# Sums of weight quarters made in HBM: the additions moved behind GpSimd's scaling steps, and one sum of the second product made on VectorE

## The chip, the cores and the metric

The kernel runs on one core of one Trainium2 chip. The metric is device time in microseconds (us), the median over the runs. Engines are named as in the profile: PE (TensorE, matrix products), ACT (ScalarE), DVE (VectorE), POOL (GpSimd) and SP (SyncE, which here only issues transfers).

## The reference

One decoder layer on 512 tokens of width 1024, in float32:

```
h = rms_norm(x); proj = h @ w_in                      # u, q, k/v for three branches, gates
y_pool = pool_mixer(u)                                # causal means over 2, 4, 8, 16 tokens
y_nsa  = nsa_mixer(q, k.., v..)                       # 16 heads: compressed + selected + window attention
merged = g_a * (y_pool @ w_proj_pool) + g_b * (y_nsa @ w_proj_nsa)
x = x + merged @ w_out
h = rms_norm(x)
x = x + square(relu(h @ w_ff1)) @ w_ff2               # w_ff1: 1024 x 4096, w_ff2: 4096 x 1024
out = rms_norm(x)
```

With 512 tokens and at most 16 selected blocks of 64, every causal block is selected, so both large attention branches are plain causal softmax. The last three lines but one, the MLP, are where the sums of this case are used; the attention is where they are made.

## The kernel before, in words

**Precision by splitting.** A float32 operand is split into a high part (ACT writes `h`) and a rest (DVE or POOL writes `l = t - h`), and a product is three matmuls: high by high, high by rest, rest by high.

**Stages.** Input projections; attention with the rest of the projections as filler between its steps (the loop at L1080); the projection `w_proj_nsa` and `w_out`; the MLP. The MLP works in four rounds `c` of 1024 hidden features each. A round has a first product (through `w_ff1`, two groups of 512 columns, class `Group`) and, in rounds 0 to 2, a second product (through `w_ff2`, two groups, class `Out`); the second product of round 3 is done plainly.

**Fewer products by sums.** Each group multiplies a 2 x 2 arrangement of quarters with seven quarter products in place of eight (the Strassen-Winograd scheme). The weights' side needs quarters and sums of quarters. With the quarters of a group called A11, A12, A21, A22, the kernel uses A11, A12, A22, S1 = A21 + A22, S3 = A11 + A21, S2 = S1 + A11 and S4 = S2 + A12 (signs are taken care of elsewhere). One quarter product is 24 matmuls of 128 x 256. The order of the products of a first product is `IN_TURN` (L138; `FIRST` in round 0), that of a second product `OUT_TURN` (L139), whose letters stand for the two groups in turn. On the activations' side, DVE and ACT make the sums T1 to T4 of the hidden quarters in `Hidden.sums`; S3 is multiplied with T3, A22 with T4, S2 with T2, A12 with hidden quarter 21, S4 with 22.

**Where the sums are made.** S1, S3 and S2 are made in HBM ahead of time, by two transfers each: SP copies one quarter into a buffer (L259, `S<-w_ff`, or `S<-S` where S2 starts from S1), and then POOL issues a transfer that adds another quarter to it (L255, `accum_op=ALU.add`). `jobs` is the list of them: three for each of the 14 groups, 42 in all. S4 is not loaded but made on DVE in the tile in which S2 was loaded (L296): the dictionary `held` keeps the first of its two terms until the other is there.

**Who issues when.** `emit_load` issues the next 512 KB load of weights on SP (L223); there are 64 loads up to the end of `w_out`, then those of the MLP. After load `i` it calls `make_sum` as often as `sums_after(i)` says: never before load 38, once for loads 38 to 40, twice for loads 41 to 51 (these are issued during attention), then after every third, and in the MLP after every fourth load. Call `n` of `make_sum` issues the addition of job `n - 2` on POOL and the copy of job `n` on SP. An addition waits on POOL until its copy has landed.

**The queues.** Every engine works through its own instructions in the order in which the compiler's scheduler has put them; an instruction whose input is not there holds all that stand behind it. In attention POOL also does, for each of 96 slots (one head, one block of queries), the scaling of the softmax (`weight`, L1007), the weights of the compressed branch (L921 to L924), half of the rests of the weights (L332) and the rotary products (L574, L577). What POOL scales in slot `i`, PE transposes (L1023) four passes of the loop later. A loaded tile (`raw`, five in the MLP: four and `raw5`) is given back for the next load when both parts have been split off.

Of the kernel before, what the change touches and what calls it, by code (L numbers as in the profile page):

```python
# [2 lines left out]

# [1 line left out]

# [11 lines left out]
ALU = mybir.AluOpType  # L17
# [45 lines left out]
def trunk(ctx: ExitStack, tc: tile.TileContext, A, out):  # L63
    nc = tc.nc
    PE, ACT, DVE, POOL = nc.tensor, nc.scalar, nc.vector, nc.gpsimd
# [39 lines left out]
    def add_key(k):  # L105
# [14 lines left out]
        else:  # L120
# [14 lines left out]
    MLP0 = len(LD)  # L135
    C_FF2 = 3
    FIRST = ("A11", "A12"), ("S1", "S3", "S2"), ("A22", "S4")
    IN_TURN = ("A11", "S3", "S1", "S2", "A12", "A22", "S4")  # L138
    OUT_TURN = ("A11", "A11", "S1", "S1", "A12", "A12", "S2", "S4", "S2", "S4", "S3", "S3", "A22", "A22")  # L139
    dp = ctx.enter_context(tc.tile_pool(name="sums", bufs=1, space=bass.MemoryType.DRAM))  # L140
    jobs, late = [], []

    def quarters(layer, c, g):

        w, r, o = ((w_f1, 0, 1024 * c + 512 * g), (w_f2, 1024 * c, 512 * g))[layer - 1]
        return {f"{i + 1}{j + 1}": w[r + 512 * j:r + 512 * j + 512, o + 256 * i:o + 256 * i + 256].rearrange(
            "(k p) c -> p k c", p=128) for i in range(2) for j in range(2)}

    def add_group(layer, c, g):

        q = quarters(layer, c, g)
        of = {"A" + k: v for k, v in q.items()}
        for o in ("S1", "S3", "S2"):
            of[o] = dp.tile([128, 4, 256], F32, name=f"{o}_{layer}{c}{g}")
        jobs.append((of["S1"], q["21"], q["22"]))
        jobs.append((of["S3"], q["11"], q["21"]))
        if late:
            jobs.append(late.pop())
        late.append((of["S2"], of["S1"], q["11"]))
        return of  # L160

    SUM_OF = {}

    def add_turn(layer, c, of, turn):
        for g, o in turn:
            key = f"{o}{layer}{c}{g}"
            if o == "S4":
                WL.append((key, key))
                continue
            if o in ("S2", "A12"):  # L170
                SUM_OF[key] = f"S4{layer}{c}{g}"
            WL.append((key, len(LD)))
            LD.append([(of[g][o], 0)])

    for c in range(4):
        of = [add_group(1, c, g) for g in range(2)]
# [6 lines left out]
        if c < C_FF2:  # L183
            of = [add_group(2, c, g) for g in range(2)]
            seen = {}
            turn = []
            for o in OUT_TURN:
                g = seen.get(o, 0)
# [10 lines left out]
    raws, hls = {}, {}  # L199
    st = {"load": 0, "prep": 0, "use": 0, "kept": 0, "pairs": 0, "sums": 0}  # L200
    spare, slots_hl = [], []
    held = {}

    def emit_load():

        i = st["load"]
        if i >= len(LD):
            return False
        segs = LD[i]
        a = segs[0][0].shape[1]  # L210
        b = sum(s.shape[2] for s, _ in segs)
        assert a * b <= 1024
        if not by_name() or st["kept"] < RAW:
            st["kept"] += by_name()
            t = wp.tile([128, 1024], F32, tag="raw", bufs=RAW, name=f"raw{i}")
        elif spare:
            t = spare.pop(0)
        else:
            return False
        st["load"] += 1  # L220
        v = t[:, :a * b].rearrange("p (a b) -> p a b", a=a)
        for s, o in segs:
            began = nc.sync.dma_start(v[:, :, o:o + s.shape[2]], s)  # L223
        raws[i] = (t, a, b)
        for _ in range(int(sums_after(i))):
            make_sum(began)
        return True

    def sums_after(i):

        p, f = len(P1), len(P1) + len(FILL2)
        if i < p + 3:
            return 0
        if i < f + 4:
            return 1 + (i >= p + 6)
        return i % 3 == 0 if i < MLP0 else i % 4 == 0

    def by_name():

        return st["load"] >= MLP0  # L240
# [5 lines left out]

    def make_sum(load):

        n = st["sums"]
        if n > len(jobs) + 1:  # L250
            return
        st["sums"] += 1
        if n > 1:
            to, _, q = jobs[n - 2]
            POOL.dma_start(to, q, accum_op=ALU.add)  # L255
        if n < len(jobs):
            to, q, _ = jobs[n]
            with tc.issue_after(load.ins):
                nc.sync.dma_start(to, q)  # L259

    part = {}
    mode = {"pool": False, "first": True}
# [201 lines left out]
    GT = ap.tile([128, NT, 48], F32, name="GT")  # L464
# [151 lines left out]
    with ExitStack() as c1:  # L616
# [185 lines left out]
        for k in P1[2:]:  # L802
            i = int(k[-1]) if k[-1].isdigit() else None
# [35 lines left out]
    with ExitStack() as c2:  # L839
# [157 lines left out]
        def weight(i):  # L997
            p, half, br, qb, h = slots[i]
            ps, sm, P = live[i]
            head = 2 * p + h  # L1000
            bl = blocks(i)
            nb_ = len(bl)
            c = 3 * head + 1 + bl[0][0]
            DVE.reciprocal(sm[:, 2, 0:nb_], sm[:, 1, 0:nb_])  # L1004
            for e, (b, o, nb) in enumerate(bl):
                n = 128 * nb
                POOL.tensor_scalar(P[:, o:o + n], P[:, o:o + n], sm[:, 2, e:e + 1], GT[:, qb, c + e:c + e + 1],  # L1007
                                   op0=ALU.mult, op1=ALU.mult)

        def pt_tile(i):  # L1010
            p, half, br, qb, h = slots[i]
# [63 lines left out]
        n = len(slots)  # L1075
# [4 lines left out]
        for i in range(n + LAG + PLAG):  # L1080
            if i < n:
                p = slots[i][0]
                if i % 12 == 3 and p + 1 < NPAIR:
                    while p + 1 not in Q:
                        fill()
                        step_side()
                if i % 12 == CMP_AT and p + 1 < NPAIR:
                    side.append(cmp_scores(p + 1))
            if i + 1 < n:
                score_pe(i + 1)  # L1090
                scored["pairs"] = (i + 2) // 12
            t = i - LAG
            if 0 <= t < n:
                turn_pe(t)
                turn_hi(t)
            if i < n:
                smax(i)
                expo(i)
            if 0 <= i - 1 < n:
                weight(i - 1)  # L1100
            if 0 <= t < n:
                turn_lo(t)
            step_side()
            want = done0 + (total - done0) * (i + 1) // (n + LAG + PLAG)
            while fdone[0] < want and fill():
                pass
            if i < 5:
                fill()
            j = t - PLAG
            if 0 <= j < n and j % 2 == 1 and pv(j):  # L1110
                o_evac(*slots[j][0:2])
# [368 lines left out]
    for c in range(4):  # L1480
# [16 lines left out]
        if c < C_FF2:  # L1497
            outs = [Out(c, h, Y) for h in range(2)]
            seen = {}
            for o in OUT_TURN:  # L1500
                h = seen.get(o, 0)
# [5 lines left out]
        else:  # L1507
# [10 lines left out]
            last = NT - 1  # L1518
            o = MA[:, 2 * last:2 * last + 2, :].rearrange("p j c -> p (j c)")
# [43 lines left out]
```

## Time and profile before

| | |
|---|---|
| median of 3 runs | 832.32 us (832.32, 828.6, 832.45) |
| the profiled execution's own time | 832.95 us |
| its span, first to last instruction | 831.1 us |
| what lies around the span | 1.85 us |
| mean granted TensorE clock | 0.987 |
| HBM read and written | 131.53 MB and 46.14 MB |

A wait row gives the waiting engine, line and tile, what released it, and then the sum in us, the number of waits and the longest. A timeline row gives start, duration, engine, line, operation, and in brackets the idle time before it and who ended it. A window row gives the length of the stretch, the busy time of PE, PE's weight loads, DVE, ACT and POOL with their number of instructions, the granted clock of TensorE, the busy share of the 16 DMA engines and GB/s. PE's matmuls overlap: a 128 x 256 one is listed with 0.28 us though the next starts about 0.12 us after it.

### The profile page before, as it was taken

The numbers are of one execution on the slowest core, as the hardware profiler recorded it, in microseconds if no ns is written. First come the engines' busy times: TensorE is split into PE (matmuls) and PEld (weight loads), VectorE is DVE, ScalarE is ACT, GpSimd is POOL, SyncE is SP. The second block draws the span as 40 slices with busy tenths as digits, with TensorE's granted clock in tenths as the row PEclk, the third lists the DMA queues.
The fourth block names the chain that finished last, engine by engine and source line by source line (L and its number), as shares of the span: only waits on it lengthen the run. The fifth ranks groups of instructions, "written<-read, shape, count | busy, mean of one in ns | idle before, by whom it ended". The sixth has DMA issues, their size and how long they took to land.

```text
span 831.1 us, 13946 instructions
## 1 busy us (share of the span) xinstructions
PE 797.0 (96%) x5081; PEld 712.2 (86%) x5081; DVE 613.8 (74%) x1195; ACT 484.0 (58%) x959; POOL 215.0 (26%) x277
## 2 busy tenths in 40 slices
PE   7999999987998999999999899999999999999997
PEld 6889878875876888888788689999999999999986
DVE  7796744535978788989565659897789778987823
ACT  6576533334976787889633447764675467436811
POOL 6000000026767788785233300010110000000000
PEclk9999999997999899999999999999999999999999
DMA  9464633389439878673696803979987944365402
GB/s 292 120 179 114 166 90 105 106 183 230 74 97 248 164 159 187 145 151 58 220 236 179 241 11 102 284 185 279 243 252 181 274 148 158 109 197 178 152 1 101
DMA packets 125502, 137.15 MB, mean 165 GB/s; under 512 B 5365, under 2 KB 112409, under 8 KB 125210
## 3 DMA queue, kind: packets, MB, share of 16 engines
q1 hardware_dynamic: 102970, 113.46, 42.7%
q0 software_dynamic: 22176, 22.02, 18.4%
q8 instruction: 40, 0.66, 0.3%
q10 hardware_dynamic: 288, 0.79, 0.3%
q14 instruction: 28, 0.23, 0.1%
HBM read 131.53 MB, written 46.14 MB: 214 GB/s over the span
## 4 chain that ended last, share of the span: by engine, by line
PE 69%; DVE 14%; DMA 5%; issue 5%; ACT 4%; POOL 3%; SPq 0%; POOLq 0%; ACTq 0%; DVEq 0%
PE psF L373 19%; PE psB L1332 16%; PE psB L373 12%; PE psB L1448 9%; DMA S<-w_ff 3%; PE psO L1057 3%; PE psT L1023 3%; PE psS L962 2%; PE psV L373 2%; DVE P L984 1%; DVE wl L287 1%; POOL wl L332 1%; PE psF L427 1%; DVE PT L1038 1%; DMA raw<-w_out 1%
## 5 line engine op out<-in xcount | busy, mean ns | idle before, releaser
L373 PE MATMUL psF<-R,wh 128*128 128x512 f32 x512 | 167.4, 405 | 0.2 <-ACT MA L820 0.2
L255 POOL DMA_DIRECT2D S<-w_ff x42 | 53.3, 1269 | 259.1 <-DMA S<-w_ff 132.4
L285 ACT ACTIVATE wh<-raw 128x1024 fp32r<-128x1024 f32 x66 | 69.7, 1057 | 76.8 <-PE psB L1448 32.5
L330 ACT ACTIVATE wh<-raw 128x512 fp32r<-128x512 f32 (+1 forms) x102 | 61.3, 619 | 84.5 <-PE psF L373 35.7
L373 PEld LDWEIGHTS psF<-R,wh 128*128 128x128 f32 x512 | 93.0, 190 | 18.1 <-ACT MA L820 0.5
L1007 POOL TENSOR_SCALAR P<-P,sm,GT 128x128 f32<-128x128 f32 (+3 forms) x128 | 99.1, 977 | 25.2 <-DVE sm L1004 17.3
L373 PE MATMUL psF<-R,wl 128*128 128x512 f32 x256 | 102.2, 399 | 0.7 <-DVE wl L332 0.7
L287 DVE TENSOR_TENSOR wl<-raw,wh 128x1024 fp32r<-128x1024 f32 x66 | 80.5, 1222 | 18.7 <-ACT wh L285 18.4
L332 DVE TENSOR_TENSOR wl<-raw,wh 128x512 fp32r<-128x512 f32 (+1 forms) x78 | 59.0, 768 | 38.1 <-ACT wh L330 37.8
L994 ACT ACTIVATE P<-P,sm 128x128 f32<-128x128 f32 (+3 forms) x128 | 71.1, 557 | 14.6 <-DVE sm L984 11.6
L984 DVE CUSTOM_DVE_ANT_0 P<-psS,cst 128x128 f32<-128x128 f32 (+3 forms) x128 | 59.7, 484 | 13.9 <-PE psT L1023 7.4
L1332 PE MATMUL psB<-R,wh 128*128 128x256 f32 x352 | 64.1, 282 | 0.0
L1034 ACT ACTIVATE PT<-psT 128x512 fp32r<-128x512 f32 (+2 forms) x96 | 49.2, 520 | 25.0 <-PE psT L1023 24.3
L1038 DVE TENSOR_TENSOR PT<-psT,PT 128x512 fp32r<-128x512 f32 (+2 forms) x96 | 56.7, 595 | 9.3 <-ACT PT L1034 8.5
L1023 PE MATMUL psT<-ident,P 128*128 128x128 f32 x320 | 52.9, 280 | 9.0 <-POOL P L1007 8.6
L373 PEld LDWEIGHTS psF<-R,wl 128*128 128x128 f32 x256 | 48.5, 190 | 11.9 <-DVE wl L332 0.9
L1023 PEld LDWEIGHTS psT<-ident,P 128*128 128x128 f32 x320 | 40.3, 143 | 20.9 <-POOL P L1007 12.8
L285 ACT ACTIVATE w3h<-raw 128x1024 fp32r<-128x1024 f32 x32 | 33.8, 1057 | 41.1 <-PE psB L1448 15.9
L1332 PEld LDWEIGHTS psB<-R,wh 128*128 128x128 f32 x352 | 54.1, 189 | 0.3 <-DVE R L1274 0.2
L332 POOL TENSOR_TENSOR wl<-raw,wh 128x512 fp32r<-128x512 f32 x28 | 41.5, 1484 | 35.3 <-ACT wh L330 35.1
L1057 PE MATMUL psO<-PT,VV 128*128 128x256 f32 x320 | 49.3, 290 | 0.4 <-ACT PT L1034 0.4
L1332 PE MATMUL psB<-R,wl 128*128 128x256 f32 x176 | 49.5, 281 | 0.0
(431 smaller groups left out, 2274.3 us busy)
## 6 DMA issues: line engine op xcount, KB each, us to landing
raw<-w_ff SPq DMA_DIRECT2D x50, 512.0 KB, 4.8
S<-w_ff POOLq DMA_DIRECT2D x42, 512.0 KB, 7.8
raw<-S SPq DMA_DIRECT2D x42, 512.0 KB, 4.6
raw<-w_in SPq DMA_DIRECT2D x32, 512.0 KB, 3.9
S<-w_ff SPq DMA_DIRECT2D x28, 512.0 KB, 6.5
S<-S SPq DMA_DIRECT2D x14, 512.0 KB, 6.0
raw<-w_proj_nsa SPq DMA_DIRECT2D x8, 512.0 KB, 4.0
raw<-w_out SPq DMA_DIRECT2D x8, 512.0 KB, 5.0
```

The lines of the kernel that those rows point to most:

```text
L285: ACT.activation(h, t, AF.Copy)
L287: DVE.tensor_tensor(l, t, h.bitcast(F32), op=ALU.subtract)
L332: eng.tensor_tensor(l[:, sl], t[:, sl], h[:, sl].bitcast(F32), op=ALU.subtract)
L373: PE.matmul(ps, a, b, start=first and j == 0, stop=last and j == n - 1, skip_group_check=True)
L984: DVE.tensor_tensor_reduce(out=P[:, o:o + n].rearrange("p (a c) -> p a c", c=128), in0=s, in1=m, scale=1.0, scalar=3e38, op0=ALU.add, op1= ...
L994: last_exp[:] = [ACT.activation(c, c, AF.Exp, bias=sm[:, 0, e:e + 1], scale=-1.0, accum_out=sm[:, 1, e:e + 1])]
L1007: POOL.tensor_scalar(P[:, o:o + n], P[:, o:o + n], sm[:, 2, e:e + 1], GT[:, qb, c + e:c + e + 1], op0=ALU.mult, op1=ALU.mult)
L1023: PE.transpose(pt[:, 128 * j:128 * j + 128], P[:, 128 * j:128 * j + 128], ident)
L1038: DVE.tensor_tensor(dL, src, dH.bitcast(F32), op=ALU.subtract)
L1057: PE.matmul(ps[:, qb % 2, :, :], VV[:, k, b, g, :], t[:, j, :, :], start=False, stop=last and j == len(kbs) - 1 and t is tL, skip_group_ch ...
L1332: PE.matmul(out, w[u][:, k, 128 * f:128 * f + 128], XB[x][v][:, k, :], **kw)
L1448: PE.matmul(out, YB[y][u][:, k, 128 * f:128 * f + 128], w[v][:, k, :], **kw)
```

## The change

The list of jobs gets shorter: groups of the second product no longer have S2 made in HBM (36 jobs, and six loads less). There S2 is made on DVE from the tiles of S3 and A22, since S2 = S1 + A11 = S3 + A22, and S4 from S2 and A12 as before. So S3 and A22 must be multiplied ahead of S2, and `OUT_TURN` puts them fifth to eighth, where A12 and S2 began before.

Copies and additions are no longer issued in one call. `make_sum` now issues only the copy and notes the job in `begun`; `add_sum` issues the addition of the oldest job begun. A copy follows each of loads 38 to 55, none the loads 56 to 63, and in the MLP every third load. In attention an addition is issued after every fourth slot where two jobs or more are begun, and it is ordered behind the last scaling step of that pass (`tc.issue_after` makes it stand behind that instruction in POOL's queue). From load 52 on, an addition goes with a load when more than two jobs are begun. Where a copy starts from a buffer whose addition is still to be issued, that addition is issued first.

```diff
-    OUT_TURN = ("A11", "A11", "S1", "S1", "A12", "A12", "S2", "S4", "S2", "S4", "S3", "S3", "A22", "A22")
+    OUT_TURN = ("A11", "A11", "S1", "S1", "S3", "S3", "A22", "A22", "S2", "A12", "S4", "S2", "A12", "S4")
...
-        for o in ("S1", "S3", "S2"):
+        for o in ("S1", "S3", "S2")[:4 - layer]:
             of[o] = dp.tile([128, 4, 256], F32, name=f"{o}_{layer}{c}{g}")
...
-        late.append((of["S2"], of["S1"], q["11"]))
+        if layer == 1:
+            late.append((of["S2"], of["S1"], q["11"]))
...
-            if o == "S4":
+            to = {"S2": "S4", "A12": "S4"}.get(o) if layer == 1 else {"S3": "S2", "A22": "S2", "S2": "S4", "A12": "S4"}.get(o)
+            if to:
+                SUM_OF[key] = f"{to}{layer}{c}{g}"
+            if o not in of[g]:
                 WL.append((key, key))
                 continue
-            if o in ("S2", "A12"):
-                SUM_OF[key] = f"S4{layer}{c}{g}"
...
-        for _ in range(int(sums_after(i))):
+        if sums_after(i):
             make_sum(began)
+        if i >= len(P1) + len(FILL2) + 4 and (len(begun) > 2 or begun and st["sums"] == len(jobs)):
+            add_sum()
...
     def sums_after(i):
-        p, f = len(P1), len(P1) + len(FILL2)
-        if i < p + 3:
-            return 0
-        if i < f + 4:
-            return 1 + (i >= p + 6)
-        return i % 3 == 0 if i < MLP0 else i % 4 == 0
+        if i < MLP0:
+            return len(P1) + 3 <= i < len(P1) + len(FILL2) + 8
+        return i % 3 == 0
...
     def make_sum(load):
-        n = st["sums"]
-        if n > len(jobs) + 1:
-            return
-        st["sums"] += 1
-        if n > 1:
-            to, _, q = jobs[n - 2]
-            POOL.dma_start(to, q, accum_op=ALU.add)
-        if n < len(jobs):
-            to, q, _ = jobs[n]
+        if st["sums"] < len(jobs):
+            to, q, _ = jobs[st["sums"]]
+            while any(q is jobs[n][0] for n in begun):
+                add_sum()
             with tc.issue_after(load.ins):
                 nc.sync.dma_start(to, q)
+            begun.append(st["sums"])
+            st["sums"] += 1
+
+    def add_sum(behind=None):
+        to, _, q = jobs[begun.popleft()]
+        with tc.issue_after(behind.ins) if behind else nullcontext():
+            POOL.dma_start(to, q, accum_op=ALU.add)
...
             if 0 <= i - 1 < n:
-                weight(i - 1)
+                last = weight(i - 1)
+            if i % 4 == 3 and len(begun) > 1:
+                add_sum(last)
```

More of the change, by code (lines that the diff above doesn't have):

```diff
@@ L1 @@
 from collections import deque
-from contextlib import ExitStack
+from contextlib import ExitStack, nullcontext
 import numpy as np
@@ L201, in trunk @@
     spare, slots_hl = [], []
-    held = {}
+    held, begun = {}, deque()
     def emit_load():
@@ L1006, in weight @@
                 n = 128 * nb
-                POOL.tensor_scalar(P[:, o:o + n], P[:, o:o + n], sm[:, 2, e:e + 1], GT[:, qb, c + e:c + e + 1],
-                                   op0=ALU.mult, op1=ALU.mult)
+                r = POOL.tensor_scalar(P[:, o:o + n], P[:, o:o + n], sm[:, 2, e:e + 1],
+                                       GT[:, qb, c + e:c + e + 1], op0=ALU.mult, op1=ALU.mult)
+            return r
         def pt_tile(i):
```

## The prediction

> **What bounds the kernel now.** I read the page first, then what PE waited for, then the busy time by stage, and last the queues of POOL and PE around each wait. The page's first part, then PE's waits:
>
> ```profile
> PE 797.0 (96%) x5081; PEld 712.2 (86%) x5081; DVE 613.8 (74%) x1195; ACT 484.0 (58%) x959; POOL 215.0 (26%) x277
> ...
> PE psT L1023 <- POOL P L1007: 8.6, 5, 2.9
> PE psB L373 <- DVE wl L332: 3.5, 1, 3.5
> PE psT L932 <- POOL PC L924: 3.3, 1, 3.3
> ```
>
> PE is the bound, and the change takes no matmul from it. What can be won is PE's idle time, 831.1 - 797.0 = 34 us, and time in which PE runs at a lower clock. Of the waits, 8.6 + 3.3 = 11.9 us end with POOL, all in attention. The stages, in windows (three stretches with waits, two without, and the MLP):
>
> ```profile
> 175.00:212.00 37.00, 28.70 (x133) 22.75 (x132) 19.41 (x62) 17.10 (x46) 21.11 (x29) 0.86 0.89 191
> 255.00:280.00 25.00, 20.44 (x115) 16.97 (x115) 19.31 (x60) 16.11 (x42) 16.19 (x22) 0.86 1.05 200
> 280.00:400.00 120.00, 118.74 (x770) 104.18 (x770) 105.85 (x346) 104.23 (x276) 89.15 (x117) 1.00 0.65 143
> 455.00:475.00 20.00, 16.48 (x64) 12.92 (x64) 12.56 (x13) 9.60 (x18) 7.77 (x6) 0.91 0.98 269
> 580.00:660.00 80.00, 79.79 (x671) 79.59 (x670) 66.21 (x79) 45.62 (x61) 6.94 (x6) 1.00 0.86 239
> 660.00:740.00 80.00, 79.80 (x671) 79.59 (x670) 69.38 (x83) 46.02 (x60) 0.00 (x0) 1.00 0.50 160
> 616.00:645.00 29.00, 28.79 (x242) 28.59 (x241) 27.88 (x37) 18.49 (x26) 2.31 (x2) 1.00 0.75 207
> ```
>
> Two stretches of early attention and one at the end of `w_out` lose time: PE idles 8.3, 4.6 and 3.5 us there, at clocks of 0.86, 0.86 and 0.91. Later attention (280 to 400) has none of that, with DVE, ACT and POOL as busy as anywhere. The MLP is full: 671 matmuls in 80 us, in one stretch with sums and in one without. So attention can gain, and the MLP can only lose. What holds POOL in the bad stretches shows in its queue, and beneath it in PE's:
>
> ```profile
> 184.77 1.15 POOL L255 DMA_DIRECT2D S<-w_ff  x1 [8.70 <-DMA S<-w_ff]
> 187.13 0.72 POOL L924 TENSOR_TENSOR PC<-cw,PC 128x256 fp32r<-128x256 f32 x1
> 195.29 1.19 POOL L255 DMA_DIRECT2D S<-w_ff  x1 [6.21 <-DMA S<-w_ff]
> 198.12 1.67 POOL L255 DMA_DIRECT2D S<-w_ff  x1
> 267.29 1.19 POOL L255 DMA_DIRECT2D S<-w_ff  x1 [4.04 <-DVE sm L1004]
> 271.67 1.19 POOL L255 DMA_DIRECT2D S<-w_ff  x1 [2.38 <-DVE PT L1038]
> 446.53 1.15 POOL L255 DMA_DIRECT2D S<-w_ff  x1 [6.08 <-DVE W1L L332]
> ...
> 187.90 0.71 PE L932 MATMUL psT<-identR,PC 128*128 128x128 f32 x4 [3.32 <-POOL PC L924]
> 197.03 0.75 PE L1023 MATMUL psT<-ident,P 128*128 128x128 f32 x2 [2.87 <-POOL P L1007]
> 200.35 0.89 PE L1023 MATMUL psT<-ident,P 128*128 128x128 f32 x2 [1.35 <-POOL P L1007]
> 269.35 0.66 PE L1023 MATMUL psT<-ident,P 128*128 128x128 f32 x4 [2.38 <-POOL P L1007]
> 273.62 0.90 PE L1023 MATMUL psT<-ident,P 128*128 128x128 f32 x3 [1.08 <-POOL P L1007]
> ```
>
> Each wait of PE comes behind an addition (L255) at which POOL stood idle: the scaling that PE needs was queued behind an addition whose copy had not landed. Where a DVE line is named (267.29, 271.67, 446.53), DVE had long been done; the copies were late. The chain of waits has the late one, the copies' landing times (issue to landing, 160 to 280 us: least, median, most) agree, and so does the list of the additions issued from 160 to 400:
>
> ```profile
> 253.47 17.66 DMA S<-w_ff
> ...
> DMA to landing us min/median/max: 4.8/6.7/17.7
> ...
> L255 POOL DMA_DIRECT2D S<-w_ff x25: 1130/1192/1717, 169.6 to 370.7; - x25
> ```
>
> **The change, part by part.**
>
> *Additions in attention.* Before, addition n - 2 is issued with copy n, and two such calls go with one load, so an addition follows its copy by a single load. In bursts that is too soon: at 252.8 two additions hung on copies of a few us before. Counting through the new code, 15 jobs are begun by load 52, and an addition goes out behind the fourth slot only where a newer job is begun: 11 to 14 additions instead of 23 up to load 51, the first four on copies issued before 190, when no slot has run yet. The 102 passes take the time from 188 to about 400, so four passes are some 8 us, longer than the 6.7 us median of a copy. The additions before the first slot, among them that of 184.77, are gone. POOL's own time for an addition, 1.19 us, falls away some ten times in attention; with POOL 89 of 120 us busy in the good stretch that is off the path and counts as nothing. If POOL were the bound it would be worth 12 us.
>
> *PE's idle time in attention.* The five waits shown are 3.32 + 2.87 + 1.35 + 2.38 + 1.08 = 11.0 us. I take all of them; the bounds are 0 (the additions wait as before) and 11.9 (all waits for POOL).
>
> *The clock.* In the two stretches PE was busy 28.70 and 20.44 us at 0.86, so (0.14 x 28.70) + (0.14 x 20.44) = 6.9 us went to the clock. From 280 to 400, where PE idles 1.3 us in 120, the clock is 1.00. Bounds 0 and 6.9; I take 4.8, nearer the upper, since the low clock stands exactly where the waits are. [...]
>
> *The end of w_out.* With loads 56 to 63 no copies go out, and no additions, so the block of 6.08 us before 446.53 is gone. The wait of 3.5 us behind it, with the clock 3.5 + 0.09 x 16.48 = 5.0 us, is the upper bound, 0 the lower, because the loads of `w_out` themselves come one tile behind another. I take 2.0.
>
> *Sums on DVE.* Six S2 sums are new, each like the S4 sums:
>
> ```profile
> L296 DVE TENSOR_TENSOR raw<-raw,raw x14: 1214/1222/1228, 515.2 to 768.3; 128x1024 f32<-128x1024 f32 x14
> ...
> 630.62 0.28 PE L1448 MATMUL psB<-wh,y21H 128*128 128x256 f32 x1
> ...
> 630.99 0.69 DVE L1390 TENSOR_TENSOR yT3L<-GB,yT3H 128x512 fp32r<-128x512 f32 x1
> 632.19 0.69 DVE L1390 TENSOR_TENSOR yT4L<-GB,yT4H 128x512 fp32r<-128x512 f32 x1
> ```
>
> That is 6 x 1.222 = 7.3 us on DVE, the upper bound. Lower bound: 0; a gain is excluded, as PE has no idle time there (79.79 of 80 us). From 616 to 645 DVE is busy 27.88 of 29 us, and the new order asks for T3 at the fifth product of a second product (start 630.62) and for T4 at the seventh, two products or 5.7 us later (80 us for 28). T3 is complete at 631.68, T4 at 632.88: T4 in time, T3's last half about when the second half of the fifth product starts, since that wants k = 0 and 1 first. The two sums at A22 fall in the same saturated stretch, where the old order had the two S4 sums. I take 0.3 us in each of three second products, 1.0 in all.
>
> *Transfers in the MLP.* Six copies, six additions and six loads go; they were hidden. But five more copies and five more additions move in between load 64 and load 120 (20 additions there instead of 15). The rows of one round with sums and one without:
>
> ```profile
> L255 POOL DMA_DIRECT2D S<-w_ff x6: 1156/1156/1158, 584.1 to 652.0; - x6
> ...
> L259 SPq DMA_DIRECT2D S<-S x3: 495/496/505, 589.1 to 645.2; - x3
> L259 SPq DMA_DIRECT2D S<-w_ff x2: 555/555/555, 599.4 to 613.9; - x2
> ...
> L223 SPq DMA_DIRECT2D raw<-S x12: 320/338/342, 581.8 to 650.9; - x12
> L223 SPq DMA_DIRECT2D raw<-w_ff x12: 367/384/392, 593.4 to 659.4; - x12
> ...
> DMA to landing us min/median/max: 3.4/5.4/7.8
> ...
> L223 SPq DMA_DIRECT2D raw<-S x12: 319/338/339, 662.3 to 731.3; - x12
> L223 SPq DMA_DIRECT2D raw<-w_ff x11: 367/383/384, 673.9 to 737.2; - x11
> ```
>
> Without sums 23 loads fill 0.50 x 80 = 40 us of DMA time, 1.74 each. With sums it is 0.86 x 80 = 68.8; less 24 x 1.74 that leaves 27 for six additions and five copies, 4.9 a pair. A first product (40 us) of the new kernel has 12 loads and 4 pairs, 20.9 + 19.6 = 40.5 us, all of it; a second product has 10 loads and 3.3 pairs, 33.6 of 40. The row of 255 to 280 shows 1.05, so it fits, with loads landing later than 5.4 us. Lower bound 0, for the same reason as above; upper bound in the rival below; I take 0.5, as loads are issued four or five ahead. The additions follow their copies by six loads there, POOL has nothing else to do, and every sum is issued at least twelve loads before it is loaded.
>
> *Sum.* -11.0 - 4.8 - 2.0 + 1.0 + 0.5 = -16.3; from the profiled execution's 832.95 us that is 816.6. The median of the runs is 0.6 below that execution, the lowest run 4.3.
>
> **The rivals.**
>
> *The clock stays low.* The waits go, but the low clock of early attention has a cause of its own, so the 4.8 us don't come back: 832.95 - 16.3 + 4.8 = 821.4. For it: the longest of the waits is 3.32 us, yet 0.86 is the mean of 37 us. Against it: the dips lie where the waits are, and nowhere from 280 to 400. Chance 0.10. [...]
>
> *The additions still wait in the burst.* The three loads from 242 to 253 bring three copies within 11 us, and copies then took up to 17.7 us. An addition behind every fourth slot can meet a copy still in flight, and the next scaling stands behind it as now. Then the stretch 255 to 280 keeps its 2.38 + 1.08 us and 70% of its 2.9 us of clock: 816.6 + 5.5 = 822.1. Chance 0.15. If all additions wait so, because the scheduler sets them as early as the order allows, nothing is won but the 2.0 of `w_out`, and the MLP's 1.5 is paid: 832.5. Chance 0.08.
>
> *Slower: the MLP waits for its loads.* In a first product four tiles rotate (one of five is held for S4), and 12 loads feed 40 us, so a tile has 4 x 3.35 = 13.4 us. Splitting takes this much of it:
>
> ```profile
> L285 ACT ACTIVATE wh<-raw 128x1024 fp32r<-128x1024 f32 x66 | 69.7, 1057 | 76.8 <-PE psB L1448 32.5
> L287 DVE TENSOR_TENSOR wl<-raw,wh 128x1024 fp32r<-128x1024 f32 x66 | 80.5, 1222 | 18.7 <-ACT wh L285 18.4
> ```
>
> The point from which it decides is a landing time of 13.4 - 2.3 = 11.1 us. With DMA full, landings of 14 us (between the 7.8 of this round and the late copy's 17.7) would give (14 + 2.3) / 4 x 12 = 48.9 us a first product, 8.7 too many, in three of them 26: 816.6 + 26 = 842.6. Against it: at 0.86 the median is 5.4. Chance 0.09.
>
> **How the numbers follow.** The forecast has 0.58, and the rest as above. A measurement of this kernel tells about 0.5% (4.2 us) from no change: faster is below 828.2, slower above 836.5. Faster: 0.58 + 0.10 + 0.15 = 0.83; same 0.08; slower 0.09. The range reaches down to all the bounds of gain, 832.95 - 11.9 - 6.9 - 5.0 = 809.2, and 2 more for the lower runs, 807; up over the two smaller gains to 829, part of the way to no gain. Left out are the cases of 832.5 and 842.6, 0.17.
>
> **What would show it.** Right: no wait of `psT L1023` or `psT L932` for POOL above 1 us; additions in attention that stand directly behind L1007 with little idle time before them; a clock of 0.95 or more from 175 to 280; attention about 14 us shorter; 671 matmuls in 80 us still in the MLP, at a DMA share of 0.9 to 1.0. Wrong: L255 with several us of idle time before it between two L1007; ACT's L285 waiting for `raw`, or PE's L1448 for DVE at the fifth to eighth product, for more than 1 us a round.

## The result, and the profile after

The changed kernel takes 826.57 us (median of 20 runs, 824.68 to 828.77), the kernel before on the same chip 830.77 (20 runs, 825.89 to 834.42): a ratio of 0.9955, interval 0.994 to 0.997. Faster, but only by 4.2 us, 0.5%, where 16.3 were forecast: the forecast is wrong, and its error is larger than the gain. The profiled execution took 825.73 us with a span of 824.0.

The page's first part, and PE's largest waits for POOL and in the MLP (us in total, times, longest; line numbers are those of the changed kernel, most of them 4 to 8 higher than before):

```profile
PE 792.6 (96%) x5081; PEld 708.5 (86%) x5081; DVE 615.0 (75%) x1201; ACT 483.5 (59%) x959; POOL 206.1 (25%) x271
```

```profile
PE psT L1028 <- POOL P L1011: 4.9, 3, 2.5
...
PE psB L1455 <- ACT wh L289: 2.7, 2, 1.4
...
PE psB L1455 <- DVE yT3L L1397: 2.0, 3, 0.8
...
PE psB L1455 <- ACT w3h L289: 1.4, 1, 1.4
```

The windows of the prediction (stretch, then busy time of PE, PEld, DVE, ACT and POOL with counts, PE's clock, DMA share, GB/s):

```profile
175.00:212.00 37.00, 33.57 (x193) 27.55 (x192) 28.27 (x89) 24.45 (x67) 24.47 (x34) 1.00 0.60 131
255.00:280.00 25.00, 24.69 (x162) 21.74 (x161) 22.84 (x78) 22.61 (x62) 17.70 (x25) 1.00 0.64 111
...
455.00:475.00 20.00, 20.00 (x96) 16.55 (x95) 12.29 (x23) 10.61 (x25) 2.29 (x2) 1.00 0.63 147
580.00:660.00 80.00, 77.86 (x638) 77.26 (x637) 65.40 (x76) 44.74 (x59) 7.78 (x7) 0.98 0.83 225
660.00:740.00 80.00, 77.86 (x650) 77.25 (x649) 69.78 (x85) 45.12 (x59) 1.50 (x2) 1.00 0.56 165
```

In the three stretches with waits PE is busy 33.57, 24.69 and 20.00 us where it was 28.70, 20.44 and 16.48, and the clock is 1.00 in each. The MLP, which was full, is full no more: 638 and 650 matmuls in 80 us where there were 671, PE idle 2.1 us in each.

The same PE pieces of the chain of waits give the account by stage, before and then after:

```profile
409.73 28.01 PE psB L373 x119
...
579.42 34.12 PE psB L1332 x287
...
659.90 34.12 PE psB L1332 x287
...
740.35 39.92 PE psB L1332 x336
```

```profile
397.86 30.73 PE psB L377 x131
...
565.38 34.11 PE psB L1339 x287
...
649.73 34.12 PE psB L1339 x287
...
732.57 39.92 PE psB L1339 x336
```

At the first row, where attention ends, the new kernel is 11.9 us ahead. In the first product of the MLP's round 0, at its first matmul with T2, the lead is 16.5 us (509.95 and 493.44 us in the chain). Then it shrinks: 14.0, 10.2 and 7.8 us at the starts of rounds 1, 2 and 3, the last three rows above. Rounds 1 and 2, in what follows the second and the third, took 80.48 and 80.45 us, now 84.35 and 82.84; the MLP gives back 2.5, 3.9 and 2.4 us, 8.7 in all (16.51 - 7.78).

The new waits lie in the first half of the second products. PE's queue in the second round, then those of ACT and DVE at the same time (start, duration, line, idle time before it and what ended it):

```profile
617.69 0.39 PE L1455 MATMUL psB<-wh,yT3L 128*128 128x256 f32 x1 [0.59 <-DVE yT3L L1397]
...
624.67 0.38 PE L1455 MATMUL psB<-w3h,yT2H 128*128 128x256 f32 x1 [1.36 <-ACT w3h L289]
625.23 0.38 PE L1455 MATMUL psB<-wh,yT4H 128*128 128x256 f32 x1 [0.18 <-DVE x L1475]
...
628.40 0.41 PE L1455 MATMUL psB<-wl,yT4H 128*128 128x256 f32 x1
```

```profile
623.56 1.06 ACT L289 ACTIVATE w3h<-raw 128x1024 fp32r<-128x1024 f32 x1 [1.90 <-DVE raw L300]
...
620.50 1.22 DVE L291 TENSOR_TENSOR wl<-raw,wh 128x1024 fp32r<-128x1024 f32 x1
621.63 0.68 DVE L1475 TENSOR_TENSOR x<-x,psB 128x512 f32<-128x512 f32 x1
622.23 1.22 DVE L300 TENSOR_TENSOR raw<-raw,raw 128x1024 f32<-128x1024 f32 x1
623.36 1.22 DVE L291 TENSOR_TENSOR wl<-raw,wh 128x1024 fp32r<-128x1024 f32 x1
624.50 0.68 DVE L1475 TENSOR_TENSOR x<-x,psB 128x512 f32<-128x512 f32 x1
```

A matmul of S2 (`yT2H`) stands ahead of the first of A22 (`yT4H`). It waits for its weights, ACT's split of S2, which waits for the new sum on DVE (L300 at 622.23). Behind it A22's first matmul waits for L1475 at 624.50, the take of S3's result: DVE reads the product out of `psB`, the PSUM bank in which PE added it up (`x<-x,psB`). DVE has no idle time between these rows. Some 1.3 us behind the waits, from 626.5 to 629.9, matmuls take 0.41 us and not 0.28, at a clock of 0.51: half clock.

### The profile page after: what moved, and what is told of

Same layout as the page of the kernel before. It is cut to its first block, busy times and chain, and to the rows that moved or that the text cites. A ratio compares the mean times of both kernels' runs of the same rounds, so it can differ in the third digit from the quotient of the medians.

```text
span 824.0 us, 13915 instructions
## 1 busy us (share of the span) xinstructions
PE 792.6 (96%) x5081; PEld 708.5 (86%) x5081; DVE 615.0 (75%) x1201; ACT 483.5 (59%) x959; POOL 206.1 (25%) x271
## 3 DMA queue, kind: packets, MB, share of 16 engines
q0 software_dynamic: 19008, 18.88, 16.3%
## 4 chain that ended last, share of the span: by engine, by line
PE 71%; DVE 16%; ACT 5%; issue 3%; DMA 2%; POOL 1%; SPq 0%; DVEq 0%; ACTq 0%; POOLq 0%
PE psF L377 21%; PE psB L1339 16%; PE psB L377 12%; PE psB L1455 9%; PE psO L1062 3%; PE psT L1028 3%; PE psS L966 2%; DVE wl L291 2%; PE psV L377 2%; DVE P L988 2%; DVE PT L1043 1%; DMA raw<-w_out 1%; PE psF L431 1%; ACT P L998 1%; PE psC L666 1%
## 5 line engine op out<-in xcount | busy, mean ns | idle before, releaser
L1011 POOL TENSOR_SCALAR P<-P,sm,GT 128x128 f32<-128x128 f32 (+3 forms) x128 | 85.6, 700 | 46.6 <-DVE sm L1008 31.0
L263 POOL DMA_DIRECT2D S<-w_ff x36 | 41.7, 1159 | 213.2 <-DMA S<-w_ff 162.0
L336 DVE TENSOR_TENSOR wl<-raw,wh 128x512 fp32r<-128x512 f32 (+1 forms) x78 | 56.1, 731 | 37.3 <-ACT wh L334 36.9
L377 PEld LDWEIGHTS psF<-R,wl 128*128 128x128 f32 x256 | 48.2, 188 | 11.9 <-DVE wl L336 0.9
L291 DVE TENSOR_TENSOR w3l<-raw,w3h 128x1024 fp32r<-128x1024 f32 x32 | 39.1, 1222 | 14.6 <-ACT w3h L289 14.6
```

Source lines behind the costliest of these rows:

```text
L291: DVE.tensor_tensor(l, t, h.bitcast(F32), op=ALU.subtract)
L336: eng.tensor_tensor(l[:, sl], t[:, sl], h[:, sl].bitcast(F32), op=ALU.subtract)
L377: PE.matmul(ps, a, b, start=first and j == 0, stop=last and j == n - 1, skip_group_check=True)
L1011: r = POOL.tensor_scalar(P[:, o:o + n], P[:, o:o + n], sm[:, 2, e:e + 1], GT[:, qb, c + e:c + e + 1], op0=ALU.mult, op1=ALU.mult)
```

## The experiments

Every kernel was timed beside the kernel before, and ratios are to that, on the same chip. Four chips were used, and the kernel before took 833.27 us on the one of `e1` to `e4`, 829.08 on that of `e5` to `e10`, 832.58 on that of `e11` to `e14` and 828.12 on that of `e15` to `e17`: a time compares with one of another group to a few us only. The lengths of rounds are read from the profiles.

**Which part loses the time.** Theory A of the first expectations: the new second product does it, with a matmul of S2 put ahead of A22's. Theory B: the denser transfers of the MLP. Theory C: chance.

`e1_issue_only`: the changed issue of copies and additions alone. S2 of the second product stays in memory (42 jobs), in the old order.

```
-    OUT_TURN = ("A11", "A11", "S1", "S1", "S3", "S3", "A22", "A22", "S2", "A12", "S4", "S2", "A12", "S4")
+    OUT_TURN = ("A11", "A11", "S1", "S1", "A12", "A12", "S2", "S4", "S2", "S4", "S3", "S3", "A22", "A22")
-        for o in ("S1", "S3", "S2")[:4 - layer]:
+        for o in ("S1", "S3", "S2"):
```

> The new issue of copies and additions alone; S2 of the second product still made in HBM (42 jobs), old order of its products. Theory A (attention gains what was forecast, and the second product loses it because the first matmul of S2 stands ahead of A22's in PE's queue): no loss in the MLP, 671 or so matmuls in 80 us, so about 12 to 13 us below the kernel before, ratio 0.984 to 0.987. Theory B (the denser transfers in the MLP cost the 8.8 us): about as the changed kernel, ratio 0.993 to 0.997. Theory C (the gain in attention was that one profiled execution's luck): ratio 0.995 to 1.0.

Measured: 818.77 us, ratio 0.9831 (0.9798 to 0.9864). Rounds take 80.46 and 80.45 us, as before, with more transfers than the changed kernel has: 24 loads in the second round at a DMA share of 0.94, and PE full.

```profile
580.00:660.00 80.00, 79.79 (x670) 79.59 (x670) 66.22 (x79) 45.62 (x60) 9.28 (x8) 1.00 0.94 256
```

B falls, and C with it; the ratio is just under A's 0.984 to 0.987. It is also the better one against the changed kernel's 0.9955, without overlap of the intervals.

`e2_second_only`: the other half. To the kernel before come only the second product's order and its sum on DVE.

```
+    OUT_TURN = ("A11", "A11", "S1", "S1", "S3", "S3", "A22", "A22", "S2", "A12", "S4", "S2", "A12", "S4")
+        for o in ("S1", "S3", "S2")[:4 - layer]:
+            to = {"S2": "S4", "A12": "S4"}.get(o) if layer == 1 else {"S3": "S2", "A22": "S2", "S2": "S4", "A12": "S4"}.get(o)
...
```

> The old issue of copies and additions, with S2 of the second product made on VectorE and its products reordered. Theory A: attention as before, each of three second products loses some 3 us, ratio 1.009 to 1.012, waits of PE at the ninth product in all three. Theory B: ratio 0.998 to 1.001, since there are fewer transfers than before.

Measured: 843.2 us, ratio 1.0103 (1.0065 to 1.0142), rounds of 84.36 and 82.85 us: the changed kernel's rounds. The MLP's loss is all in this half.

`e3_order_only`: the order alone, S2 loaded from memory as before.

> The old issue, S2 still made in HBM and loaded, only the order of the second product's products is the new one. In PE's queue the first matmul of S2 stands ahead of A22's here too. Theory A in its form A1 (the split of S2 needs the slot that S3's last matmul gives back, so whoever makes the sum PE waits some 1.4 us): ratio 1.006 to 1.012. Form A2 (the sum on a saturated VectorE comes too late): no wait, ratio 0.999 to 1.002, but for the wait for T3 (0.6 us each).

Measured: 835.72 us, ratio 1.0039 (1.0012 to 1.0067), rounds of 82.22 and 82.25 us. So the order costs 1.8 us a round by itself, without the S2 sum on DVE (the S4 sums are there, as before). The ratio lies between the two forms. PE waits 1.2 us a round for the split of S2, nearly as A1 had it, though S2 was loaded.

`e4_pinned`: the changed kernel, with S2's matmuls held behind the last matmul of the product before them.

```
+                with tc.issue_after(pinned[0].ins) if o == "S2" else nullcontext():
+                    r = PE.matmul(out, YB[y][u][:, k, 128 * f:128 * f + 128], w[v][:, k, :], **kw)
+                if o != "S2":
+                    pinned[:] = [r]
```

> The changed kernel with S2's matmuls in the second product held behind the last matmul before them in PE's queue (order only, nothing computed otherwise). Theory A: the waits of 1.4 + 0.2 us and the half clock behind them go in all three second products, 2.4 to 3.3 us each, 7 to 9 us in all: ratio to the kernel before 0.984 to 0.988, about 819 us. Theory B (transfers) and A2 (the sum on VectorE is late): no more than 1 us better than the changed kernel, ratio 0.994 to 0.997.

Measured: 828.89 us, ratio 0.9955 (0.993 to 0.9979), rounds of 84.53 and 83.07 us: nothing won. The matmul of S2 is gone from there, and the wait stays, 2.0 us where it was 1.36 + 0.18, now openly for the take. PE's waits, its row in the second round, and DVE's queue:

```profile
PE psB L1458 <- DVE x L1480: 6.0, 3, 2.0
```

```profile
629.83 0.36 PE L1458 MATMUL psB<-wh,yT4H 128*128 128x256 f32 x1 [2.00 <-DVE x L1480]
...
626.72 1.22 DVE L300 TENSOR_TENSOR raw<-raw,raw 128x1024 f32<-128x1024 f32 x1
627.86 1.22 DVE L291 TENSOR_TENSOR wl<-raw,wh 128x1024 fp32r<-128x1024 f32 x1
629.00 0.68 DVE L1480 TENSOR_TENSOR x<-x,psB 128x512 f32<-128x512 f32 x1
```

A falls as to the place of that matmul. A new theory, D: A22 accumulates in the PSUM bank that holds S3 (`X`, with `AFTER` A22 on S3), so its first matmul waits until DVE's take has read S3. In either order just one product, 2.9 us (a round of 80 us has 28), lies between S3 of a group and its A22; but the old order has them at the end of the second product, the new one in its middle, where DVE works without a pause on T's sums and splits. The sum of S2 stands in that queue as well.

**Testing D.** `e5_pool_sum`: `e4_pinned` with the sum of S2 on POOL.

```
-            DVE.tensor_tensor(t, t, held[to], op=ALU.add)
+            (POOL if to.startswith('S22') else DVE).tensor_tensor(t, t, held[to], op=ALU.add)
```

> The kernel of e4_pinned, with the S2 sums of the second product on GpSimd instead of VectorE. Theory D (VectorE's queue is full in the first half of each second product: the take of S3 stands behind T's splits and behind the sum of S2, and A22, which accumulates in S3's PSUM bank, waits for that take): two sums of 1.22 us leave VectorE's queue, so PE's wait of 2.0 us a round for x (the take of S3) falls to under 1 us, rounds go from 84.5 and 83.1 us to 82 to 83.2, in all 823 to 827 us where e4_pinned had 828.9. Rival E (the order alone is what costs, the sums are covered): the wait stays at 1.5 us or more, rounds over 83, 827.5 to 830. Rival F (GpSimd's own sum is late for the split of S2, or its addresses clash with VectorE): waits of L1458 for wh or raw appear, over 830.

Measured: 831.56 us, ratio 1.003 (1.0007 to 1.0053), rounds of 85.24 and 83.76 us. The wait for the take grows from 2.0 us to 2.7 in the second round and up to 3.5 in the others. F is nearest, by its time and in that DVE is slow beside POOL (a clash of addresses is its guess, the rows show the times alone): while POOL adds, DVE's split takes 3.07 us in place of 1.22, so DVE's queue is no shorter. The split ends 1.1 us after POOL's sum, about as if it had started only then. But the wait that grows is the one D names. POOL's sum, then DVE's queue:

```profile
625.58 2.37 POOL L300 TENSOR_TENSOR raw<-raw,raw 128x1024 f32<-128x1024 f32 x1 [1.90 <-DVE wl L291]
...
625.97 3.07 DVE L291 TENSOR_TENSOR wl<-raw,wh 128x1024 fp32r<-128x1024 f32 x1
628.96 1.27 DVE L1480 TENSOR_TENSOR x<-x,psB 128x512 f32<-128x512 f32 x2
```

`e6_own_bank`: `e4_pinned` with A22 in a bank of its own. The take of S3 then subtracts in two places, one more DVE operation for each S3.

```
-             "S3": ("c", "T3"), "A22": ("c", "T4")}
-        AFTER = {"A12": "A11", "S4": "S1", "A22": "S3"}
+             "S3": ("c", "T3"), "A22": ("e", "T4")}
+        AFTER = {"A12": "A11", "S4": "S1"}
+            if o == "S3":
+                x = self.quarter(1, 0)
+                DVE.tensor_tensor(x, x, ps.rearrange("p (t c) -> p t c", t=2), op=ALU.subtract)
```

> The kernel of e4_pinned, with A22 in a PSUM bank of its own: A22 no longer waits for the take of S3, at the price of one more VectorE subtraction for each S3 (two a round, about 0.6 us each). The sums stay on VectorE, the order stays new. Theory D: PE's waits for x (2.0 us a round, and the half clock behind them) are gone, rounds 81 to 82.8 us, in all 819 to 825 us. Rival E (what costs is T3 arriving late and VectorE's total work; the bank is only where it shows): the wait moves to yT3L, yT4L or wl, rounds stay above 83.3, 827 to 831.

Measured: 821.49 us, ratio 0.9907 (0.9875 to 0.994), rounds of 81.61 and 81.64 us. The wait for the take is gone though DVE has more to do, as D has it.

`e11_own_bank_free`: the same edit on the changed kernel, without `e4_pinned`'s order.

> The changed kernel with one edit: A22 of the second product in a PSUM bank of its own (the edit of e6_own_bank, without e4_pinned's order for S2's matmuls). Theory D (the wait for the take of S3 is what the second products lose): rounds of 81 to 82 us and 819 to 823 us in all, as e6_own_bank's 821.5. Rival A (once that wait is gone, S2's first matmul, which the schedule puts ahead of A22's, waits for its split w3h): PE waits for w3h of 1.4 us a round stay, rounds of 82.5 to 84, 824 to 828 us.

Measured: 819.38 us, ratio 0.9838 (0.9814 to 0.9863), rounds of 80.76 and 80.78 us, a little under D's 81 to 82. Of PE's waits in the second round only T3's is left, and the clock is 1.00. No matmul of S2 is put ahead of A22's any more; A22's first follows S3's last at once:

```profile
PE psB L1455 <- DVE yT3L L1397: 0.6, 1, 0.6
```

```profile
621.05 0.28 PE L1455 MATMUL psB<-w3h,yT3L 128*128 128x256 f32 x1
621.17 0.28 PE L1455 MATMUL psB<-wh,yT4H 128*128 128x256 f32 x1
```

```profile
580.00:660.00 80.00, 79.41 (x668) 79.20 (x667) 68.83 (x82) 45.32 (x60) 8.12 (x7) 1.00 0.90 241
```

`e14_order_and_bank`: `e1_issue_only` with the new order and the bank, that is without the sum on DVE.

> The kernel of e1_issue_only (S2 of the second product loaded from memory, 42 jobs) with the new order of the second product and A22 in a bank of its own. Against e6_own_bank it lacks only the two S2 sums of 1.22 us on VectorE in each second product, against e1_issue_only it has only the order. Theory D (VectorE's queue is full there, so each sum still delays T's splits and the weights' after the bank is set free): rounds of 80.5 to 81.2 us, 817.5 to 820.5 us. Rival (the sums are covered once A22 needn't wait; the 1.1 us a round that e6_own_bank has over 80.46 are T3's): rounds of 81.4 to 81.9, 820.5 to 823 us.

Measured: 818.36 us, ratio 0.9831 (0.9806 to 0.9856), rounds of 80.79 and 80.80 us. It fits D's range, but not D's reason: with the bank free the sum costs nothing (80.76 with it, 80.79 without). It is covered, as the rival said; the rival's 81.4 to 81.9 were too high, since most of the 1.1 us over 80.46 belonged to the pinned order (`e11_own_bank_free` is at 80.76).

**Which part of the issue wins attention's time.** Theory P: the order behind the scaling step. Theories Q and N: the number of copies and additions, or the gap between them.

`e9_unordered`: `e1_issue_only` with `add_sum()` in place of `add_sum(last)`.

> The kernel of e1_issue_only, with the additions at every fourth slot not ordered behind the scaling step. Theory P (the order behind the scaling is what takes the waits for GpSimd away): additions again stand ahead of a scaling step and wait for their copies there, PE's waits psT for POOL come back to 6 us or more, 824 to 831 us. Theory Q (fewer copies and a longer gap between a copy and its addition do it; the order is cover only): waits for POOL stay under 6 us in all, 816 to 821, as e1_issue_only's 818.8.

Measured: 821.97 us, ratio 0.9901 (0.9866 to 0.9936). Waits for POOL are back at 4.6 + 3.3 us, as P had it and more than Q allowed, but the time lies between the two ranges, above Q's 821 and below P's 824.

`e10_fewer_copies`: the copies of `e1_issue_only`, each addition with the second copy after its own, as before.

> The kernel of e1_issue_only with its copies (one for each load in attention, every third load in the MLP), but an addition issued with the second copy after its own, as before, at no slot and behind no scaling step. Theory P (order behind the scaling, and so an addition at every fourth slot): additions stand ahead of scalings with their copies under way, waits for POOL of 8 us or more, 827 to 833 us. Theory Q (half as many jobs a load, which alone doubles the gap between copy and addition): 818 to 823 us. If the number of additions in attention alone counts for GpSimd's time, it lies near e1_issue_only's 818.8.

Measured: 819.43 us, ratio 0.9885 (0.9848 to 0.9921), as Q had it, with waits for POOL of 4.8 us in all.

`e12_wider_gap`: the kernel before, the addition with the fourth copy after its own. `e13_few_and_late`: the same on `e10_fewer_copies`; in it one sum, S2 of the third round's second product, is loaded before its second operand is added, so that kernel leaves this operand out of its product.

```
-            if len(begun) > 2:
+            if len(begun) > 4:
                 add_sum()
```

> The kernel before with one thing changed: an addition goes out with the fourth copy after its own instead of the second. Copies are as many and as dense as before (two for each load in attention), the additions as many. Theory G (the gap between copy and addition decides): the waits for GpSimd in attention, 11.9 us before, fall under 6 us, the clock from 255 to 280 us is 0.95 or more, 817 to 824 us. Theory N (their number decides: the transfers fill the queues at a DMA share of 1.0, copies come late by more than the gap, or GpSimd's 1.2 us for each addition tells): waits for GpSimd of 7 us or more, 826 to 833 us.

> The kernel of e10_fewer_copies (one copy for each load in attention) with the addition at the fourth copy after its own instead of the second. Theory G: the idle time of 5.95 us ahead of the addition at 192 us goes, and with it PE's wait of 3.58 us behind it; 814 to 818 us. Theory N: as e10_fewer_copies, 818 to 821 us, since a gap of two loads is enough for all copies but the first few.

Measured: 833.0 us, ratio 1.0 (0.9977 to 1.0022), and 822.78 us, ratio 0.9881 (0.9859 to 0.9903). The first is N's time, the second lies above both theories' ranges, but neither edit widened the gap. In POOL's queue the additions stand in nearly the same places: in `e12_wider_gap` the fourth after 160 us at 193.41 after 6.63 us idle, before at 195.29 after 6.21 (its profiled execution is its fastest, 826.58 us). `e13_few_and_late` has its additions within 1 us of those of `e9_unordered`. In these kernels the schedule puts an addition early, wherever the program writes it; only the order behind a scaling moved it. So theory G, a wider gap without that order, stays untested.

Three kernels were then run on one chip, which with the kernel before make a table of two by two. `e15_dense_ordered` has before's copies, and the additions behind the scaling of every second slot:

```
-            if i % 4 == 3 and len(begun) > 1:
+            if i % 2 == 1 and len(begun) > 1:
                 add_sum(last)
```

> The copies and their number as in the kernel before (two for each load in attention, 42 jobs, the old order of the second product), the additions behind the scaling step of every second slot. It fills the fourth field of a table: dense and free is the kernel before, few and free is e17_few_unordered, few and behind the scaling is e16_few_ordered. Theory P (the order is what counts): 818 to 823 us, waits for GpSimd 5 us or less. Theory N (the number of copies and additions in the stretches of dense transfers is what counts): 827 to 833 us, with the stretch from 255 to 280 us still at a DMA share of 1.0 and PE busy less than 22 of 25 us. Both count about half: 823 to 827.

> The kernel of e1_issue_only once more, beside the two others on one chip: 817 to 821 us by every theory, a ratio of 0.980 to 0.988.

> The kernel of e9_unordered once more, beside e16_few_ordered on one chip. Theory P+N (order is worth something even with few copies, since the first additions at 186 and 197 us stood idle 8.67 and 6.24 us before they could go, and attention ended 5.0 us later than in e1_issue_only): 3 to 5 us above e16_few_ordered. Theory N: within 1.5 us of it, the difference of the two earlier runs being that of two chips.

| copies for each load in attention | additions free | behind the scaling |
|---|---|---|
| two | before: 828.12 | `e15_dense_ordered`: 823.25, ratio 0.9948 (0.9922 to 0.9973) |
| one | `e17_few_unordered`: 821.74, ratio 0.9922 (0.9906 to 0.9939) | `e16_few_ordered`: 817.8, ratio 0.9876 (0.9858 to 0.9893) |

Both count: the order wins 4.9 and 3.9 us, fewer copies 6.4 and 5.5 us. `e15_dense_ordered` falls into the range of "both count about half", `e17_few_unordered` into that of P+N. Waits for POOL are not all that the order changes: in `e15_dense_ordered` they are still 8.0 us, more than P's 5. That row, the windows of `e15_dense_ordered`, and then those of `e17_few_unordered`:

```profile
PE psT L1029 <- POOL P L1012: 8.0, 5, 3.8
```

```profile
175.00:212.00 37.00, 32.81 (x179) 26.93 (x179) 26.05 (x79) 22.95 (x61) 23.76 (x32) 0.95 0.76 176
255.00:280.00 25.00, 23.13 (x151) 19.84 (x150) 22.42 (x76) 20.75 (x57) 20.22 (x27) 1.00 1.08 230
```

```profile
175.00:212.00 37.00, 29.27 (x135) 23.18 (x135) 17.55 (x62) 16.84 (x45) 20.44 (x27) 0.86 0.76 154
255.00:280.00 25.00, 24.65 (x164) 21.77 (x163) 22.71 (x76) 20.70 (x57) 16.67 (x24) 1.00 0.51 106
```

The order alone mends most of the early stretch (PE busy 32.81 us instead of 28.70) and over half of the late one (23.13 instead of 20.44). With few copies and no order the early stretch is as bad as before (29.27 of 37 us, clock 0.86) and the late one is good; there the DMA share is 0.51 instead of 1.05. In the early one POOL still stands idle at additions, and PE behind them:

```profile
185.78 1.15 POOL L261 DMA_DIRECT2D S<-w_ff  x1 [8.92 <-DMA S<-w_ff]
196.35 1.19 POOL L261 DMA_DIRECT2D S<-w_ff  x1 [6.25 <-DMA S<-w_ff]
...
188.91 0.53 PE L934 MATMUL psT<-identR,PC 128*128 128x128 f32 x4 [3.55 <-POOL PC L926]
198.09 0.75 PE L1026 MATMUL psT<-ident,P 128*128 128x128 f32 x2 [2.86 <-POOL P L1009]
```

Two limits of the table. "One copy for each load" also means none with loads 56 to 63, so part of what it wins lies at the end of `w_out`: in the profiles `e16_few_ordered` is ahead of `e15_dense_ordered` by 4.0 us where attention ends and by 5.9 at the start of the second round. And the order is not the only way: `e10_fewer_copies` has none, and its attention ends at 398.75 us, with `e16_few_ordered` at 398.49 and `e17_few_unordered` at 402.77. Its profiled execution, 816.94 us, is its fastest, and its median of 819.43 is from another chip; why it does better than `e17_few_unordered` stays open.

## Why the prediction was wrong, by its steps

*Sums on DVE: the step that failed.* The term was 1.0 us with a bound of 7.3; the MLP gave back 8.7, over the bound, and none of it through the transfers (`e1_issue_only`). The step asked whether T3 and T4 would be there in time, and they were, all but 0.6 us a round, 2.0 in three. It priced the sums by their own 1.22 us. What it left out is that the new order puts A22, which accumulates in S3's bank, into the stretch where DVE has no idle time, so that the take of S3 is late. The text had read just that stretch (27.88 of 29 us busy) and asked only who waits for T and the sums, not who waits for the other entries of that queue. The runs split the second round's 3.9 us: T3's wait with the new order 0.3 (80.79 against 80.46), the shared bank 1.4 (82.22 against 80.79), the sum in the queue ahead of the take 2.1 (84.35 against 82.22). Of that 2.1, some 1.5 are the half clock: the third round has the same waits, stays at a clock of 1.00 and takes 82.84. With the bank freed, 0.3 is left of all of it (80.76).

*PE's idle time in attention and the clock: most of it came, in part for another reason.* 11.0 + 4.8 = 15.8 forecast; attention ends 11.9 us earlier, 13.4 without the 1.5 us by which this execution's first transfers came later (the chain's first 24 products of `psF` begin at 21.30 us, before at 19.81). The clock is 1.00 in both stretches, so the rival of a clock with another cause falls (0.95 and 1.00 in `e16_few_ordered`); only between them, from 212 to 255 us, it is 0.96 where it was 1.00. PE's waits for POOL fell from 11.9 to 4.9 us, by 7.0 and not by 11.0. One of the five waits, the 1.35 us at 200.35, did not fit the reading from the start: the addition ahead of it, at 198.12, has no idle time before it. The prediction counted on fewer additions and on four passes between a copy and its addition. In the table of two by two about half of the gain goes with the order and half with the lower number of copies, though `e10_fewer_copies` had nearly all of it without the order; the late stretch is mended by the number alone, as 255 to 280 us shows in `e17_few_unordered`, and that a wider gap helps by itself is not shown. "No wait of `psT L1023` above 1 us" was wrong: 4.9 us in three waits are left. They are POOL's own work, for which nothing was counted. Ahead of the longest but one, POOL goes through scalings, an addition and rotary products without a pause:

```profile
189.41 2.81 POOL L1011 TENSOR_SCALAR P<-P,sm,GT 128x128 f32<-128x128 f32 x6
192.17 1.26 POOL L263 DMA_DIRECT2D S<-w_ff  x1
193.05 1.84 POOL L578 TENSOR_TENSOR rx<-rx,cst 128x256 f32<-128x256 f32 x2
194.45 1.79 POOL L581 TENSOR_TENSOR rs<-rs,cst 128x256 f32<-128x256 f32 x2
195.84 2.30 POOL L1011 TENSOR_SCALAR P<-P,sm,GT 128x256 f32<-128x256 f32 x3
...
196.82 0.44 PE L1028 MATMUL psT<-ident,P 128*128 128x128 f32 x2 [2.16 <-POOL P L1011]
```

*The rival of additions that still wait* was half right: the scheduler does set each as early as it may, but the order allows no earlier place, and no addition of the changed kernel up to 285 us has idle time before it.

*The end of `w_out`:* 16.5 - 11.9 = 4.6 us won, near the upper bound of 5.0 and not the 2.0 taken.

*Transfers in the MLP:* 0 rather than 0.5, as `e1_issue_only` shows at a DMA share of 0.94; the slower rival, loads that land late, did not come.

*The base.* The sum was made against the profiled execution, 832.95 us. That was 2.2 above the median of 20 runs, and after's profiled one 0.8 below its own. Profile to profile the gain is 7.2 us, between the medians 4.2. By stage the profiles have -11.9 - 4.6 + 8.7 = -7.8 us, where the prediction had -15.8 - 2.0 + 1.5 = -16.3.

"Wrong: PE's L1448 for DVE at the fifth to eighth product, for more than 1 us a round" named the place. It was given no price of its own, and so no rival. That 826.57 us lies inside the stated 807 to 829 is luck: the upper end stood for smaller gains in attention, and no case of the prediction has the gain there and a loss in the second products.

## What to carry to other kernels

When an edit moves work into a stretch where an engine has no idle time, list every entry of that engine's queue there and who waits for each; a read that frees a PSUM bank is such an entry (2.0 us of PE's time a round in `e4_pinned`), and a second bank can cost less than the wait (rounds of 81.61 and 81.64 us in `e6_own_bank`, 84.53 and 83.07 in `e4_pinned`). Price a wait of PE with the clock that the trace shows behind it (some 1.5 us in the second round here, nothing in the third). Two changes that go together are worth trying apart: the first half of this one gives a ratio of 0.9831 without the second, and with one more bank both together give 0.9838, so the second is nearly free there and wins nothing.

## What the runs showed of the hardware

In the second round of `e4_pinned` a wait of 2.00 us on PE was followed by 3.5 us at a clock of 0.51, and by (1 - 0.51) x 3.5 that is an estimated 1.7 us more; the round is 1.5 us longer than the third, which has such a wait and a clock of 1.00 (84.53 and 83.07 us). PE waits 2.00 us before 629.83, runs ten matmuls at a clock of 1.00, and then:

```profile
628.00:631.00 3.00, 1.18 (x10) 1.21 (x11) 3.00 (x4) 1.06 (x1) 0.00 (x0) 1.00 0.66 191
631.00:634.50 3.50, 3.50 (x20) 3.50 (x19) 1.75 (x3) 0.16 (x1) 0.00 (x0) 0.51 0.66 211
634.50:640.00 5.50, 5.50 (x48) 5.50 (x48) 4.40 (x5) 1.96 (x2) 1.17 (x1) 1.00 0.35 102
```

In the changed kernel 3.4 us at 0.51 (626.5 to 629.9) stand behind waits of 1.36 and 0.18 us around a single matmul. In the third round of `e4_pinned` a wait of 2.0 us leaves the clock at 1.00, and so does one of 1.2 us in both rounds of `e3_order_only`. In attention, too, like waits cost unlike amounts: from 255 to 280 us PE idles 5.9 us in the profile of `e12_wider_gap` at a clock of 1.00, and 4.6 us in that of the kernel before at 0.86. What decides whether the clock falls behind a wait, these runs do not show.

POOL held up DVE in `e5_pool_sum`: two 128x1024 subtractions on DVE took 3.07 and 2.42 us beside POOL sums of 2.37 and 2.38 us, against 1.21 to 1.23 for those with no sum on POOL beside them (616 to 640 us of that profile), and each ended 1.1 us after its sum. What the two engines contend for, the run does not show.
